# Batch norm with ReLU: the first half of x loaded and stored in pieces of 1, 1, 2, 4 and 8 rows per partition instead of 2, 2, 4 and 8

## The chip, the cores and the metric

One core of one Trainium2 chip; the sessions used different chips. The metric is the device time of one execution in microseconds. Timed runs of two kernels are taken in turns on the same chip. Executions of one kernel mostly lie within 0.3 us of each other.

## The reference

```python
batch, channels, h, w = 32, 128, 32, 32          # x: float32, 16.78 MB
normalized = (x - running_mean) / np.sqrt(running_var + eps)     # per channel
return np.maximum(normalized * gamma + beta, 0)
```

x is read once and the result written once, 33.56 MB in all. Per element there is one multiplication, one addition and a maximum.

## The kernel before

x is seen as 4096 rows of 1024 numbers, in two halves; each partition has 16 rows (J) of a half. A load brings some rows of every partition, 4 KB each and contiguous in memory; a store sends them back.

```python
J = 16
PIECES = (((0, 2), (2, 4), (4, 8), (8, 16)), ((0, 8), (8, 16)))
...
    for t in range(T):                              # T = 2 halves
        for a, b in PIECES[t]:
            xt = data.tile([P, b - a, HW], F32, name=f"x{t}_{a}")
            nc.sync.dma_start(out=xt, in_=xr[t, :, a:b, :])
            tiles.append((t, a, b, xt))
    raw = params.tile([Q, 4, J], F32, name="raw")
    for k, src in enumerate((running_var, gamma, running_mean, beta)):
        nc.scalar.dma_start(out=raw[:, k, :], in_=src.rearrange("(q j) -> q j", j=J))
    ...                                             # matmul, sqrt, reciprocal: scale_t, bias_t
    for t, a, b, xt in tiles:
        for j in range(a, b):
            nc.scalar.activation(out=xt[:, j - a, :], in_=xt[:, j - a, :], func=ACTF.Relu,
                                 bias=bias_t[:, j : j + 1], scale=scale_t[:, j : j + 1])
        nc.scalar.dma_start(out=outr[t, :, a:b, :], in_=xt)
```

All pieces have their own buffers, so no load waits for a buffer (before loads of x, the sync engine waited only for the landings of gamma, 3.1 us, and of beta, 0.9 us). Loads are issued from the sync engine (SP), parameter loads and stores from the scalar engine (ACT).

## Time and profile before

| | before |
|---|---|
| median time, 6 runs | 84.27 us |
| span in the profile | 82.3 us |
| scalar engine busy | 38.2 us |
| first activation, first store issued | 9.38, 11.78 us |
| last load landed, last store issued | 51.2, 60.39 us |
| first and last data packet of the DMA engines | 1.81, 81.10 us |

Times inside a profile count from the span's start. In the 40 slices, a digit is the busy share in tenths; in the stretches, the last two columns are the mean busy share of the 16 DMA engines and what they moved in GB/s. A packet is counted, in slices and stretches alike, with all its time in the one in which it begins, so a share can pass 1. A line of a timeline gives start, length, engine, line of the kernel, operation, what is written <- what is read, and the count; in brackets stands how long the engine had been idle and what ended that. SPq and ACTq are the DMA issues of these engines. A load is called landed when the activation that waits for it is released, about 1 us after its last packet (51.2 and 50.2 us here). "Packet records" below are the trace's single DMA packets, each with queue, start, duration and size. A "packet" there is one contiguous row of a piece, so its size is the piece's rows times 4 KB (before: 256 load packets of 8 KB, 128 of 16 KB and 384 of 32 KB, and as many store packets).

### The profile page before, as it was taken

How to read it: one execution, taken by the hardware profiler on the slowest of the kernel's cores; microseconds unless marked ns; L12 is line 12 of the kernel's file. 1: busy time of each engine (PE TensorE's matmuls, PEld its weight loads, DVE VectorE, ACT ScalarE, POOL GpSimd, SP SyncE). 2: the span in 40 equal slices, each digit the busy share in tenths (PEclk: the TensorE clock that was granted, in tenths of full speed). 3: DMA queues.
4: the chain of work that ended last, by engine and by line, in shares of the span. 5: the costliest groups of instructions: out<-in, count | busy, mean ns of one | idle time of the engine just before them, and what ended most of it. 6: DMA issues, size and time to landing. Idle time of an engine off the chain costs nothing.

```text
span 82.3 us, 117 instructions
## 1 busy us (share of the span) xinstructions
PE 0.7 (1%) x2; PEld 0.5 (1%) x2; DVE 0.8 (1%) x5; ACT 38.2 (46%) x34; POOL 0.8 (1%) x6
## 2 busy tenths in 40 slices
PE   0003000000000000000000000000000000000000
PEld 0002000000000000000000000000000000000000
DVE  0000300000000000000000000000000000000000
ACT  0600599990009999509999401999930000000000
POOL 3000000000000000000000000000000000000000
DMA  2899999997998997997999898997998999799790
GB/s 36 315 431 486 398 486 398 462 430 319 462 526 351 462 430 327 582 430 319 446 510 446 382 382 374 518 478 303 494 494 366 414 510 446 319 510 478 303 494 0
DMA packets 1792, 33.56 MB, mean 408 GB/s; under 512 B 256, under 2 KB 256, under 8 KB 256
## 3 DMA queue, kind: packets, MB, share of 16 engines
q1 hardware_dynamic: 864, 16.78, 48.6%
q10 hardware_dynamic: 928, 16.78, 47.5%
HBM read 16.78 MB, written 16.78 MB: 408 GB/s over the span
## 4 chain that ended last, share of the span: by engine, by line
DMA 60%; ACT 10%; ACTq 1%; issue 1%
DMA x<-in_x_dram 53%; ACT x L92 10%; DMA raw<-in_beta_dram 6%; ACTq L57 1%
## 5 line engine op out<-in xcount | busy, mean ns | idle before, releaser
L92 ACT ACTIVATE x<-x,bias_t,scale_t 128x1024 f32<-128x1024 f32 x32 | 36.6, 1227 | 15.4 <-DMA x<-in_x_dram 14.4
L80 ACT ACT_TABLE_LOAD x1 | 1.3, 1283 | 2.7 <-issue 2.7
L80 ACT ACTIVATE std_t<-cols,eps_t 128x16 f32<-128x16 f32 x1 | 0.3, 273 | 4.1 <-PE cols L72 4.1
L72 PE MATMUL cols<-raw,rep 8*128 8x64 f32 x2 | 0.7, 428 | 7.4 <-DMA raw<-in_beta_dram 7.4
L72 PEld LDWEIGHTS cols<-raw,rep 8*128 8x128 f32 x2 | 0.5, 306 | 7.4 <-issue 7.4
L62 POOL TENSOR_SCALAR_AFFINE_SELECT rep<-rep 8x128 f32<-8x128 f32 x1 | 0.4, 393 | 0.1
L82 DVE RECIPROCAL rstd_t<-std_t 128x16 f32<-128x16 f32 x1 | 0.3, 253 | 7.5 <-ACT std_t L80 7.5
L61 POOL MEMSET rep<- 8x128 f32 x1 | 0.2, 194 | 0.3 <-POOLq L116 0.3
L84 DVE TENSOR_TENSOR scale_t<-cols,rstd_t 128x16 f32<-128x16 f32 x1 | 0.2, 175 | 0.1
L86 DVE TENSOR_TENSOR ms_t<-cols,scale_t 128x16 f32<-128x16 f32 x1 | 0.2, 175 | 0.0
L88 DVE TENSOR_TENSOR bias_t<-cols,ms_t 128x16 f32<-128x16 f32 x1 | 0.2, 175 | 0.0
L116 POOL MEMSET const-bfloat16-1.0<- 128x1 bf16 x1 | 0.1, 106 | 0.0
L116 POOL MEMSET const-uint8-127<- 128x1 uint8 x1 | 0.1, 106 | 0.0
L116 POOL MEMSET const-float32-0.0<- 128x1 f32 x1 | 0.1, 103 | 0.3 <-issue 0.3
L116 POOL MEMSET const-float32-1.0<- 128x1 f32 x1 | 0.1, 103 | 0.0
L59 DVE MEMSET eps_t<- 128x1 f32 x1 | 0.1, 59 | 0.9 <-PEq L116 0.9
## 6 DMA issues: line engine op xcount, KB each, us to landing
x<-in_x_dram SPq DMA_DIRECT2D x3, 4096.0 KB, 22.7
out_dram<-x ACTq DMA_DIRECT2D x3, 4096.0 KB, 21.0
x<-in_x_dram SPq DMA_DIRECT2D x2, 1024.0 KB, 6.0
x<-in_x_dram SPq DMA_DIRECT2D x1, 2048.0 KB, 11.4
out_dram<-x ACTq DMA_DIRECT2D x2, 1024.0 KB, 25.9
out_dram<-x ACTq DMA_DIRECT2D x1, 2048.0 KB
raw<-in_running_var_dram ACTq DMA_DIRECT2D x1, 0.5 KB
raw<-in_gamma_dram ACTq DMA_DIRECT2D x1, 0.5 KB
```

The costliest lines, as they stand in the source:

```text
L57: nc.scalar.dma_start(out=raw[:, k, :], in_=src.rearrange("(q j) -> q j", j=J))
L59: nc.vector.memset(eps_t, float(eps))
L61: nc.gpsimd.memset(rep, 1.0)
L62: nc.gpsimd.affine_select(out=rep, in_=rep, compare_op=mybir.AluOpType.is_equal, fill=0.0, base=0, pattern=[[0, P // Q], [-1, Q]], channel ...
L72: nc.tensor.matmul(cols.rearrange("p k j -> p (k j)"), rep.rearrange("q r s -> q (r s)"), raw.rearrange("q k j -> q (k j)"), start=True, s ...
L80: nc.scalar.activation(out=std_t, in_=cols[:, 0, :], func=ACTF.Sqrt, bias=eps_t[:, 0:1], scale=1.0)
L82: nc.vector.reciprocal(out=rstd_t, in_=std_t)
L84: nc.vector.tensor_mul(out=scale_t, in0=cols[:, 1, :], in1=rstd_t)
L86: nc.vector.tensor_mul(out=ms_t, in0=cols[:, 2, :], in1=scale_t)
L88: nc.vector.tensor_sub(out=bias_t, in0=cols[:, 3, :], in1=ms_t)
L92: nc.scalar.activation(out=xt[:, j - a, :], in_=xt[:, j - a, :], func=ACTF.Relu, bias=bias_t[:, j : j + 1], scale=scale_t[:, j : j + 1],)
L116: nc = _bacc.Bacc("TRN2", target_bir_lowering=False, num_devices=1)
```

## The change

The intent: the first piece lands sooner, its activation and its store start sooner, and loads and stores run side by side for longer.

```diff
-PIECES = (((0, 2), (2, 4), (4, 8), (8, 16)), ((0, 8), (8, 16)))
+PIECES = (((0, 1), (1, 2), (2, 4), (4, 8), (8, 16)), ((0, 8), (8, 16)))
```

## The prediction

That the two queues take turns packet by packet is read from the trace of the kernel before: gamma, mean and beta landed at 5.98, 6.62 and 7.26 us, about two packets of 0.309 us apart, and beside 32 KB load packets the first store's 8 KB packets began in groups about 1.5 us apart (16.00, 17.53, 19.11, 20.63 us).

> **What bounds the kernel now.** I read the page first: the engine totals, the 40 slices, the chain; then the timeline of the scalar engine, the busy time by stretches, and last the records of single DMA packets, because the page pointed to the DMA. The page, and the chain that ended last:
>
> ```profile
> PE 0.7 (1%) x2; PEld 0.5 (1%) x2; DVE 0.8 (1%) x5; ACT 38.2 (46%) x34; POOL 0.8 (1%) x6
> ...
> ACT  0600599990009999509999401999930000000000
> POOL 3000000000000000000000000000000000000000
> DMA  2899999997998997997999898997998999799790
> ...
> HBM read 16.78 MB, written 16.78 MB: 408 GB/s over the span
> ...
> DMA 60%; ACT 10%; ACTq 1%; issue 1%
> ```
>
> The scalar engine, the only compute engine with work, is idle for more than half of the span; the DMA row shows no gap from the second slice (2 us) to the last but one (80 us). The chain runs through a DMA most of the time. The stretches say whether the DMA engines ever had nothing to do (columns: stretch, length, busy time of PE, PEld, DVE, ACT and POOL, clock, DMA share, GB/s; a packet is booked where it ends, so a share can pass 1):
>
> ```profile
> 2.00:10.00 8.00, 0.66 (x2) 0.49 (x2) 0.78 (x4) 2.17 (x3) 0.00 (x0) 1.00 1.00 413
> 10.00:16.00 6.00, 0.00 (x0) 0.00 (x0) 0.00 (x0) 6.00 (x6) 0.00 (x0) 1.00 0.96 400
> 16.00:37.00 21.00, 0.00 (x0) 0.00 (x0) 0.00 (x0) 11.70 (x12) 0.00 (x0) 1.00 1.04 443
> 37.00:51.20 14.20, 0.00 (x0) 0.00 (x0) 0.00 (x0) 9.16 (x8) 0.00 (x0) 1.00 0.97 412
> 51.20:60.40 9.20, 0.00 (x0) 0.00 (x0) 0.00 (x0) 9.16 (x8) 0.00 (x0) 1.00 1.05 454
> 60.40:80.00 19.60, 0.00 (x0) 0.00 (x0) 0.00 (x0) 0.00 (x0) 0.00 (x0) 1.00 1.00 431
> 80.00:82.30 2.30, 0.00 (x0) 0.00 (x0) 0.00 (x0) 0.00 (x0) 0.00 (x0) 1.00 0.00 0
> ```
>
> The share is 0.96 to 1.05 in every stretch from 2 to 80 us, whether only loads run (up to 16 us), both (to 51 us) or only stores (after), and the rate does not depend on which. So loads and stores share one budget, and **the kernel is bound by its DMA engines from the first packet to the last**. The packet records give the budget exactly. Each piece is 128 packets, 8 on each of 16 engines, one per partition. Loads and stores take the same time for the same size (median): 8 KB 0.309 us, 16 KB 0.611 us, 32 KB 1.213 us. One engine's loads are 8 x (2 x 0.309 + 0.611 + 3 x 1.213) = 38.9 us; with the stores 77.9 us. The first data packet starts at 1.8 us, the last ends at 81.1 us: 79.3 us, of which only 1.4 us is anything but packets at their usual pace (slow first packets, some slower 32 KB reads).
>
> The scalar engine's timeline shows when stores are issued:
>
> ```profile
> 9.38 3.50 ACT L92 ACTIVATE x<-x,bias_t,scale_t 128x1024 f32<-128x1024 f32 x3 [1.03 <-DVE bias_t L88]
> 11.78 0.38 ACTq L99 DMA_DIRECT2D out_dram<-x  x1
> ...
> 37.00 1.24 ACT L92 ACTIVATE x<-x,bias_t,scale_t 128x1024 f32<-128x1024 f32 x1 [2.97 <-DMA x<-in_x_dram]
> 37.00 0.34 ACTq L99 DMA_DIRECT2D out_dram<-x  x1
> ...
> 51.21 1.24 ACT L92 ACTIVATE x<-x,bias_t,scale_t 128x1024 f32<-128x1024 f32 x1 [5.05 <-DMA x<-in_x_dram]
> 51.21 0.34 ACTq L99 DMA_DIRECT2D out_dram<-x  x1
> ...
> 60.39 0.34 ACTq L99 DMA_DIRECT2D out_dram<-x  x1
> ```
>
> The first activation starts at 9.38 us, released by bias_t, the end of the parameter chain; the first piece of x had landed at 5.7 us. So the size of the first piece is not what holds the first activation. A store also comes just after the first activation of the next piece, so two stores (37.00, 51.21) wait 3 and 5 us for the next load; that costs nothing, as the DMA is busy with loads.
>
> [...] 33.56 MB in 79.3 us is 423 GB/s, a steady 32 KB packet gives 16 x 32768 B / 1.213 us = 432 GB/s, for loads and stores together. [...] beside 32 KB loads, an 8 KB store packet should get one turn in 0.309 + 1.213 = 1.52 us, so 8 turns take 12.2 us; the first store's packets run from 16.0 to 27.6 us (11.6 us). [...]
>
> **The change, part by part.** It replaces one 1 MB load by two of 512 KB, and one 1 MB store likewise. Every byte still moves once, the activations stay 32 of 1.225 us.
>
> Packets: 4 KB ones were never measured here. The three sizes lie on a line: 0.302 us for 8 KB more, 0.602 us for 16 KB more, which leaves 0.007 us per packet. So a 4 KB packet is estimated at 0.158 us. Per engine, 8 packets of 8 KB (2.47 us) become 16 of 4 KB (2.53 us): +0.06 us for the load, +0.06 us for the store, and 2 completion packets of 0.009 us: **+0.13 us on the path that sets the end.**
>
> Issues: one more on the sync queue (about 0.43 us) and one more on the scalar queue (0.34 us). The loads' issues (0.43 us apart) stay ahead of the 512 KB pieces' transfer (8 x 0.158 = 1.3 us each), so no engine runs dry. Hidden.
>
> Parameters: the four parameter loads take turns with packets of x. Gamma, mean and beta land 0.64 us apart, which is two turns behind 8 KB packets each. Behind 4 KB packets they come sooner; beta, now at 7.3 us, I expect at 5 to 6.8 us, the first activation at 7 to 9 us instead of 9.38, the first store, now one activation later instead of two, at 8.3 to 10.2 us instead of 11.78. That is the intended effect, about 2.5 us. It is not on the path: until the loads end, an earlier store packet only takes a turn from a load packet.
>
> Loads and stores between: small store packets get fewer bytes per turn. Before, some 16 packets of 8 KB and 5.4 of 16 KB (8.2 us per engine) went out before the last load packet ended at 50.2 us. Now each of about 22 remaining 32 KB load packets shares with a store packet: 16 of 0.158 and 6 of 0.309 us, 4.4 us. So the last load should land some 3.8 us sooner, at about 47.4 us instead of 51.2, and the last store be issued at about 56.6 instead of 60.39 us. **This gain is not kept**: the bytes that the stores did not move by then remain to be moved. After the loads (46.4 us), 38.97 + 0.06 - 4.4 = 34.6 us of store packets remain, which ends at 81.0 us plus small gaps, as now. And the store queue cannot run dry: when the loads end, about 15 us of earlier stores are queued (a few of the 2-row piece, the 4-row piece 4.9 us, the 8-row piece 9.7 us), the next store is issued within a microsecond, and the last one 10 us later.
>
> Sum: 84.28 + 0.13 = **84.4 us**.
>
> **The rivals.** (1) *The earlier start shortens the end.* If the store stream were a pipeline of its own, with its own bandwidth, a store 2.5 us earlier would give 81.8 us (3% faster). For it: the change was made for that. Against it: the DMA share of 0.96 to 1.05 in all stretches and the same 0.309 and 1.213 us in both directions; a third of the time in load-only and store-only phases would leave room if directions were separate, and the rate does not rise when both run. (2) *Small packets are slow.* If a 4 KB packet took as long as an 8 KB one, the 32 added packets' worth would cost 2 x 8 x 0.15 = 2.4 us: 86.8 us, 3% slower. For it: never measured here[...]. Against it: the 0.007 us intercept. (3) *A new wait on a reused semaphore.* The fifth and sixth loads wait for the landing of parameter loads (issued at 6.00 and 7.27 us), since the kernel seems to have eight DMA semaphores. One more load and one more store shift these pairs; a store that waits for a late load would hold the scalar queue. With 10 us or more of queued packets behind every issue after 7 us this would have to be a very long wait: perhaps 0 to 1 us. (4) *The first microseconds.* The first packet of x took up to 1.17 us instead of 0.31 us; with half-size packets such a start-up could be a few tenths better or worse.
>
> **Range and chances.** Rivals 1 and 2 each need a linear or a saturated row of this trace to break: 1.5% each. Rivals 3 and 4 move the time by tenths; the three runs before spread over 0.3 us. So 84.0 to 84.9 us eight times in ten; faster by over 2% 0.015, within 2% 0.97, slower by over 2% 0.015.
>
> **What would show it.** Right: DMA share near 1 in all stretches from 2 to 80 us; 4 KB packets near 0.16 us; first store before 10.5 us; last load landing near 47.4 and last store issue near 56.6 us, and yet the last packet at 81 us. Wrong: a hole in the DMA row (rival 3), 4 KB packets well above 0.16 us (rival 2)[...].

## The result

The changed kernel's median is 84.41 us (84.15 to 84.48, 6 runs) against 84.27 us (84.13 to 84.46, 6 runs): ratio 1.001, 95% interval 0.999 to 1.003. In a second comparison in a later session (below) it was 1.0028 (1.0012 to 1.0044). So the change gains nothing; by the medians it costs 0.14 and 0.20 us, and only the second is clear of noise.

From the page of the changed kernel: the activity of ACT and DMA in 40 slices, and the chain that ended last.

```profile
ACT  0600489993019999289995099993000000000000
...
DMA  1999999897979697969889799998999899799980
...
DMA 55%; ACT 10%; issue 1%; SPq 1%; ACTq 0%
```

The last busy slice of ACT moved from the 30th to the 28th (two slices are 4 us): the scalar engine is done sooner. The DMA row still ends in the 39th. The changed kernel's stretches, with the same columns and bounds as those of before:

```profile
2.00:10.00 8.00, 0.66 (x2) 0.50 (x2) 0.78 (x4) 1.95 (x3) 0.00 (x0) 1.00 1.00 385
10.00:16.00 6.00, 0.00 (x0) 0.00 (x0) 0.00 (x0) 5.55 (x6) 0.00 (x0) 1.00 1.05 453
16.00:37.00 21.00, 0.00 (x0) 0.00 (x0) 0.00 (x0) 14.17 (x13) 0.00 (x0) 1.00 0.99 422
37.00:51.20 14.20, 0.00 (x0) 0.00 (x0) 0.00 (x0) 11.38 (x11) 0.00 (x0) 1.00 1.01 436
...
60.40:80.00 19.60, 0.00 (x0) 0.00 (x0) 0.00 (x0) 0.00 (x0) 0.00 (x0) 1.00 1.00 431
```

No stretch has a hole. In the first the share is 1.00, as before, but only 385 GB/s moved instead of 413: the packets take longer there (0.83 us of excess per engine against 0.44 us, in the budget below). The scalar engine's timeline:

```profile
9.61 2.37 ACT L92 ACTIVATE x<-x,bias_t,scale_t 128x1024 f32<-128x1024 f32 x2 [1.02 <-DVE bias_t L88]
10.88 1.50 ACTq L99 DMA_DIRECT2D out_dram<-x  x2
...
47.30 1.24 ACT L92 ACTIVATE x<-x,bias_t,scale_t 128x1024 f32<-128x1024 f32 x1 [2.82 <-DMA x<-in_x_dram]
...
56.48 0.34 ACTq L99 DMA_DIRECT2D out_dram<-x  x1
```

The first store is issued 0.9 us sooner, the last load lands 3.9 us sooner, the last store is issued 3.9 us sooner, and the last data packet ends at 81.11 us instead of 81.10. What the middle gained is given back at the end, where the stores that did not go out earlier still have to go out. The profiled run was the fastest of the six (84.15 us); in the second profile (84.63 us) the last load landed at 48.04 us, the last store was issued at 57.23 us and the last packet ended at 81.59 us.

An early issue is also not an early store: the first store's first packet began at 14.85 us, 4.0 us after the issue (before: 16.00 us, 4.2 us after). In e6 below, where the loads had just ended, it was 0.9 us (41.19 to 42.07 us).

### The profile page after: what moved, and what is told of

It reads as the page before. It is cut to its first block, busy times and chain, and to the rows that moved or that the text cites. A ratio compares the mean times of both kernels' runs of the same rounds, so it can differ in the third digit from the quotient of the medians.

```text
span 82.4 us, 121 instructions
## 1 busy us (share of the span) xinstructions
PE 0.7 (1%) x2; PEld 0.5 (1%) x2; DVE 0.8 (1%) x5; ACT 38.3 (46%) x34; POOL 0.8 (1%) x6
## 3 DMA queue, kind: packets, MB, share of 16 engines
q10 hardware_dynamic: 1072, 16.78, 47.4%
## 4 chain that ended last, share of the span: by engine, by line
DMA 55%; ACT 10%; issue 1%; SPq 1%; ACTq 0%
DMA x<-in_x_dram 55%; ACT x L92 10%; SPq L50 1%; ACTq L99 0%
```

## The experiments

**Theory:** the end is the start of the first packet, plus the time of all packets of one DMA engine, plus the stalls of packets, plus the holes in which the engines have nothing. When a store or an activation starts matters only if it opens a hole. **Rivals:** (R1) stores run as a stream of their own, so their start matters; (R2) what happens beside the loads is hidden, only the part after the last load counts; (R3) the number of transfers or the activations set the end.

### e1: the first half's stores held back by 22 us (from the changed kernel)

```diff
+    held = []
     for t, a, b, xt in tiles:
         for j in range(a, b):
-            nc.scalar.activation(...)
-        nc.scalar.dma_start(out=outr[t, :, a:b, :], in_=xt)
+            act = nc.scalar.activation(...)
+            if held and t == 1:
+                with tc.issue_after(act.ins):
+                    for o, i in held:
+                        nc.scalar.dma_start(out=o, in_=i)
+                held = []
+        if t == 0:
+            held.append((outr[t, :, a:b, :], xt))
+        else:
+            nc.scalar.dma_start(out=outr[t, :, a:b, :], in_=xt)
```

> The changed kernel with the same pieces, but all stores of the first half of x held back until after the first activation of the second half, so that the first store is issued at about 33 us instead of 10.9 us. Theory (the DMA engines' packet time alone sets the end): no hole arises, because the last load still runs; the loads end sooner (last landing near 43 us), the stores follow back to back, time 84.3 to 84.6 us, within 0.3% of the kernel before. Rival (the moment of the first store matters, stores form a stream of their own): the stores start 22 us later, so the end comes well later, above 90 us.

Measured: 85.03 us (84.94 to 85.09, 4 runs), before 84.20; ratio 1.0092 (1.0077 to 1.0107). The first store was issued at 33.07 us:

```profile
33.01 1.24 ACT L93 ACTIVATE x<-x,bias_t,scale_t 128x1024 f32<-128x1024 f32 x1 [0.55 <-DMA x<-in_x_dram]
33.07 2.35 ACTq L103 DMA_DIRECT2D out_dram<-x  x5
```

R1 falls: 22 us of delay cost 0.6 us against the changed kernel's 84.41 (another session). But 0.6 us is outside what the theory expected. The packet records show the 32 KB load packets 0.59 us per engine slower than their usual 1.213 us in total, all of it between 35 and 45 us, after these stores were issued; in the changed kernel it was 0.14 us. There is no hole.

### e2: the opposite of the change, the first half in two pieces of 8 rows (from the kernel before)

```diff
-PIECES = (((0, 2), (2, 4), (4, 8), (8, 16)), ((0, 8), (8, 16)))
+PIECES = (((0, 8), (8, 16)), ((0, 8), (8, 16)))
```

> The opposite of the change: the first half of x in two pieces of 8 rows, as the second half. First store near 23 us instead of 11.8. Theory: 24 packets fewer of 8 and 16 KB per engine and direction, replaced by 32 KB ones: 8 x (1.229 - 1.213) = 0.13 us less per direction, so 84.0 us (83.8 to 84.3), no hole. Rival (the first store's moment matters): 8 to 11 us slower.

Measured: 84.99 us (84.87 to 85.09, 4 runs), ratio 1.0087 (1.0071 to 1.0103). The first store came at 24.06 us, 12 us later than before, and cost 0.8 us, not 8 to 11. Again R1 falls, and again the theory's figure was too low by about 1 us. Its stretches around the first store:

```profile
24.00:26.00 2.00, 0.00 (x0) 0.00 (x0) 0.00 (x0) 1.54 (x3) 0.00 (x0) 1.00 1.40 524
26.00:28.00 2.00, 0.00 (x0) 0.00 (x0) 0.00 (x0) 2.00 (x3) 0.00 (x0) 1.00 0.95 246
28.00:30.00 2.00, 0.00 (x0) 0.00 (x0) 0.00 (x0) 2.00 (x2) 0.00 (x0) 1.00 0.69 295
```

Packets are booked where they begin, so take the three together: the share is (1.40 + 0.95 + 0.69) / 3 = 1.01, so the engines were busy, but they moved (524 + 246 + 295) / 3 = 355 GB/s. The records show why: load packets that began between 25.4 and 27.6 us took up to 1.8 us longer than 1.213 us, 1.17 us per engine in all. So in this kernel load packets stall after the first store's issue at 24.06 us and before its first packet at 28.79 us. The share of busy time hides it; the rate shows it.

### e3: 4 KB packets for every transfer (from the kernel before)

```diff
-            xt = data.tile([P, b - a, HW], F32, name=f"x{t}_{a}")
+            xt = data.tile([P, b - a, HW + 16], F32, name=f"x{t}_{a}")[:, :, :HW]
```

> The kernel before with its own pieces, but with 64 bytes of padding behind each row of x in the on-chip buffers, so that every transfer goes in 4 KB packets. Same transfers, same waits, same activations. Theory: 256 packets of 0.159 us per engine and direction are 40.7 us against 38.94, so 3.5 us more: 87.8 us (87.3 to 88.6), 4% slower. Rival (the end is set by the number of transfers, their issue or the activations): 84.3 us. Rival (small packets cost more in bulk than the first 16 per engine showed): above 89 us.

Measured: 86.43 us (86.35 to 86.49, 4 runs), ratio 1.0258 (1.0243 to 1.0273). Same transfers and activations, 2.2 us slower: the packets' time sets the end, and R3 falls. But the expected 3.5 us were too many. Its stretches, first with loads and stores, then with stores alone:

```profile
20.00:60.00 40.00, 0.00 (x0) 0.00 (x0) 0.00 (x0) 18.56 (x17) 0.00 (x0) 1.00 1.02 421
62.00:82.00 20.00, 0.00 (x0) 0.00 (x0) 0.00 (x0) 6.91 (x7) 0.00 (x0) 1.00 1.02 422
```

and the kernel before with stores of 32 KB packets alone:

```profile
62.00:79.00 17.00, 0.00 (x0) 0.00 (x0) 0.00 (x0) 0.00 (x0) 0.00 (x0) 1.00 1.00 432
```

A steady share of 1.02 says that recorded packets overlap by some 2%: a 4 KB packet is recorded with 0.159 us but one follows the other every 16 x 4096 B / 422 GB/s = 0.155 us. At 422 instead of 432 GB/s, 33.55 MB need 79.5 instead of 77.7 us, 1.8 us more; that is most of the 2.2 us. The step that failed was to multiply recorded durations by the count.

### e5: the first two stores left out (from the kernel before; wrong result)

```diff
-        nc.scalar.dma_start(out=outr[t, :, a:b, :], in_=xt)
+        if (t, a) not in ((0, 0), (0, 2)):
+            nc.scalar.dma_start(out=outr[t, :, a:b, :], in_=xt)
```

> Wrong result on purpose: the kernel before without its first two stores (rows 0 to 3 of the first half, 2 x 1 MB, never written). Theory: these stores' 16 packets of 0.309 us per engine are on the path that sets the end although they go out beside loads in the first half of the span: 4.94 us less, 79.3 us (79.0 to 79.6). Rival (stores beside loads are hidden, only what comes after the last load counts): 84.3 us.

Measured: 80.92 us (80.79 to 81.17, 4 runs), ratio 0.9611 (0.9587 to 0.9634), so 3.3 us less. R2 falls: these 2 MB go out beside loads, before 40 us, and taking them away shortens the end. The missing 1.6 us are a hole, in the stretches around 57 us:

```profile
50.00:56.00 6.00, 0.00 (x0) 0.00 (x0) 0.00 (x0) 0.00 (x0) 0.00 (x0) 1.00 1.01 437
56.00:57.00 1.00, 0.00 (x0) 0.00 (x0) 0.00 (x0) 0.00 (x0) 0.00 (x0) 1.00 0.02 0
57.00:58.00 1.00, 0.00 (x0) 0.00 (x0) 0.00 (x0) 0.67 (x1) 0.00 (x0) 1.00 0.00 0
58.00:59.00 1.00, 0.00 (x0) 0.00 (x0) 0.00 (x0) 1.00 (x2) 0.00 (x0) 1.00 1.22 524
```

```profile
57.33 1.24 ACT L92 ACTIVATE x<-x,bias_t,scale_t 128x1024 f32<-128x1024 f32 x1 [10.19 <-DMA x<-in_x_dram]
57.39 0.34 ACTq L100 DMA_DIRECT2D out_dram<-x  x1
```

The store of the second 4 MB piece stands in the scalar engine's queue behind the first activation of the last piece, which waits until 57.33 us for its load. All earlier stores were done by then, so the DMA engines idled (1.6 us of all engines, by the records). Expected gain 4.94 us less 1.6 us is 3.3 us, as measured. (Load packets also stalled 0.4 us more than before, 0.98 against 0.56 us; terms of 0.1 to 0.3 us at the start and the end offset most of that.) This is the same queue order that cost nothing in the kernel before, where stores stood behind waits of 2.97 and 5.05 us; here, where the store queue ran dry, it cost the 1.6 us.

### e4: the parameter loads ahead of x on the sync queue (from the kernel before)

```diff
+    raw = params.tile([Q, 4, J], F32, name="raw")
+    for k, src in enumerate((running_var, gamma, running_mean, beta)):
+        nc.sync.dma_start(out=raw[:, k, :], in_=src.rearrange("(q j) -> q j", j=J))
     tiles = []
...
-    raw = params.tile([Q, 4, J], F32, name="raw")
-    for k, src in enumerate((running_var, gamma, running_mean, beta)):
-        nc.scalar.dma_start(out=raw[:, k, :], in_=src.rearrange("(q j) -> q j", j=J))
```

> The kernel before with the four parameter loads moved from the scalar engine's queue to the sync engine's, ahead of the loads of x. The parameters land some microseconds sooner (by about 4 us instead of 7.3), so the first activation starts as soon as the first piece of x lands, near 7.5 us instead of 9.4; but the first load of x is issued about 1.5 us later. Theory (first x packet + packet time = end): 1.3 to 1.7 us slower, 85.8 us. Rival (the start of the activations and of the stores counts): up to 2 us faster, 82.5 us.

Measured: 85.61 us (85.40 to 85.77, 4 runs), before 84.21; ratio 1.0165 (1.0146 to 1.0185), so 1.4 us more. Its timeline:

```profile
2.24 5.17 SPq L53 DMA_DIRECT2D x<-in_x_dram  x6
...
7.15 3.63 ACT L92 ACTIVATE x<-x,bias_t,scale_t 128x1024 f32<-128x1024 f32 x3 [2.80 <-DMA x<-in_x_dram]
```

The activations start 2.2 us sooner than before (7.15 against 9.38 us), yet the kernel is slower by just what the first load is later: 2.24 - 0.81 = 1.43 us. The first data packet moved from 1.81 to 3.22 us, 1.41 us.

### e6: each half in one piece of 16 rows (from the kernel before)

```diff
-PIECES = (((0, 2), (2, 4), (4, 8), (8, 16)), ((0, 8), (8, 16)))
+PIECES = (((0, 16),), ((0, 16),))
```

> Each half of x in one piece of 16 rows: two loads and two stores of 8 MB. The first store can be issued only when 16 activations are done after the first landing near 22 us, that is near 41 us, just when the loads end (40.8 us), and the second near 61 us, just when the first store's packets end. Theory: packet time falls by 0.3 us or more, but two holes of 0 to 1.5 us each in the DMA row can open: 84 to 86.5 us, and the packet records account for the difference as holes. If larger pieces only ever gain: 83.8 us. Rival (the first store's moment matters as such): over 100 us.

Measured: 83.70 us (83.61 to 83.88, 6 runs), before 84.21; ratio 0.9938 (0.9924 to 0.9953). The first store was issued at 41.19 us, 29 us later than before, and the kernel is 0.5 us faster. That is below the expected 84 to 86.5 us. Where the loads end:

```profile
41.00:42.00 1.00, 0.00 (x0) 0.00 (x0) 0.00 (x0) 0.16 (x1) 0.00 (x0) 1.00 0.01 0
42.00:43.00 1.00, 0.00 (x0) 0.00 (x0) 0.00 (x0) 0.80 (x1) 0.00 (x0) 1.00 2.45 1049
```

The records show one hole, between 41 and 43 us, worth 0.8 us, and not the second that was allowed for. After the start the load packets lose only 0.01 us, and loads and stores never meet (the first store packet began at 42.07 us, after the loads); that gain was not expected. (The profiled run, 83.88 us, was the slowest of the six, so its last packet, at 80.99 us, shows only part of the 0.5 us.)

### h1: loads of before, stores of after

```diff
+STORES = (((0, 1), (1, 2), (2, 4), (4, 8), (8, 16)), ((0, 8), (8, 16)))
...
     for t, a, b, xt in tiles:
-        for j in range(a, b):
-            nc.scalar.activation(...)
-        nc.scalar.dma_start(out=outr[t, :, a:b, :], in_=xt)
+        for c, d in STORES[t]:
+            if c < a or d > b:
+                continue
+            for j in range(c, d):
+                nc.scalar.activation(...)
+            nc.scalar.dma_start(out=outr[t, :, c:d, :], in_=xt[:, c - a : d - a, :])
```

> One half of the change: loads as before (2, 2, 4, 8 rows), stores as after (1, 1, 2, 4, 8 rows). What the runs so far suggest: each engine's load packets stall just before the first store packets, the more the larger that first store is (summed over time, per engine: 0.14 us with 512 KB in the changed kernel, 0.38 us with 1 MB before, 0.95 us with 2 MB, 1.17 us with 4 MB), and the first microseconds of the loads cost 0.44 us with 8 KB packets but 0.84 us with 4 KB ones. If so, this half keeps the gain alone: 0.2 us less than before, 83.9 to 84.1 us, excess of the load packets near 0.6 us. Rival (both are chance differences of single profiles): 84.2 to 84.3 us, as before.

Measured: 83.74 us (83.71 to 83.91, 6 runs), before 84.17; ratio 0.9946 (0.9923 to 0.9969). That is below the expected 83.9 to 84.1 us; the excess of the load packets, 0.57 us, was near the expected 0.6. The gain over the kernel before is clear of noise.

### h2: loads of after, stores of before

```diff
+LOADS = (((0, 1), (1, 2), (2, 4), (4, 8), (8, 16)), ((0, 8), (8, 16)))
...
-            nc.sync.dma_start(out=xt, in_=xr[t, :, a:b, :])
+            for c, d in LOADS[t]:
+                if a <= c and d <= b:
+                    nc.sync.dma_start(out=xt[:, c - a : d - a, :], in_=xr[t, :, c:d, :])
```

> The other half: loads as after (1, 1, 2, 4, 8 rows), stores as before (2, 2, 4, 8 rows). By the same theory this half keeps the loss alone: 0.4 us more than before, 84.5 to 84.7 us, start-up excess of the 4 KB load packets near 0.8 us. Rival (chance): 84.2 to 84.4 us.

Measured: 84.33 us (84.25 to 84.45, 6 runs), ratio 1.0010 (0.9989 to 1.0030). A miss: the loss at the start was there (0.81 us of excess), but the later excess, expected as before, was only 0.12 us.

### h3: the loads of e2 with the stores of after

```diff
-PIECES = (((0, 2), (2, 4), (4, 8), (8, 16)), ((0, 8), (8, 16)))
+PIECES = (((0, 8), (8, 16)), ((0, 8), (8, 16)))
+STORES = ...                                       # and the loop of h1
```

> Loads of the first half in two pieces of 8 rows as in the second experiment (84.99 us), but stores in pieces of 1, 1, 2, 4 and 8 rows. Theory (the stall at the first store grows with its size): the stall falls from 1.17 us to 0.1 to 0.4 us and the time to 84.0 to 84.3 us. Rival (any first store beside a load stream of 32 KB packets costs that stall): 84.9 to 85.0 us.

Measured: 84.37 us (84.19 to 84.51, 6 runs), ratio 1.0011 (0.9988 to 1.0033); e2 was at 1.0087, on another chip. The time is just above the expected range. The gain over e2 is there, 0.6 us. At the first store (19 to 21 us) the stall fell from 1.17 to about 0.22 us; another 0.61 us came between 41 and 44 us, in the last load packets, which the theory of a stall at the first store doesn't explain.

### e9: loads and stores kept apart, made to be the fastest

```diff
-PIECES = (((0, 2), (2, 4), (4, 8), (8, 16)), ((0, 8), (8, 16)))
+PIECES = (((0, 2), (2, 16)), ((0, 16),))
+STORES = (((0, 2), (2, 16)), ((0, 8), (8, 16)))
...                                                  # the loop of h1; the store of rows 0 and 1
+            with tc.issue_after(act.ins):           # queued behind the activation of row 15
+                for o, i in held:
+                    nc.scalar.dma_start(out=o, in_=i)
```

> A version meant to be the fastest: 64 KB packets nearly throughout, first load small, no store before about 39 us, when the loads are about to end, so that loads and stores hardly meet; the last store split so that it is issued in time. Theory: first packet at 1.8 us, 77.4 us of packets, 0.45 us at the start, 0.2 to 0.5 us where stores begin, no hole: 82.8 to 83.4 us, 1.0 to 1.6% faster than before, although its first store comes 27 us later. If the stores were held too long a hole opens at 41 us as in the run with whole halves: 83.7 us. Rival (late stores cost): above 84.5 us.

Measured: 84.54 us (84.49 to 85.12, 6 runs), ratio 1.0045 (1.0018 to 1.0073). It failed, in two ways that its timeline shows:

```profile
20.21 5.88 ACT L98 ACTIVATE x<-x,bias_t,scale_t 128x1024 f32<-128x1024 f32 x5 [1.02 <-DVE bias_t L90]
24.98 0.38 ACTq L110 DMA_DIRECT2D out_dram<-x  x1
26.00 12.53 ACT L98 ACTIVATE x<-x,bias_t,scale_t 128x1024 f32<-128x1024 f32 x11
```

By the kernel's text the store of rows 0 and 1 stands behind 16 activations, but it was issued when the fifth began, with 11 of the 16 still to start. (The trace doesn't record the order of the built program. But the semaphore wait of the second store, whose rows need all 16, ran at 25.41 us, with the same 11 to start.) So its place in the text did not make the store wait for those 16 activations, and stores met the loads after all. Nor did it go as soon as its own rows were done, at about 22.6 us (an estimate: 20.21 us plus 2.37 us, which two activations take in the changed kernel); why it went at 24.98 us isn't shown. And the parameter loads, taking turns with 56 KB packets, landed so late that the matmul that waits for beta started at 18.23 us and the first activation at 20.21 us. (How long such turns are, the records show later in this run: 8 KB store packets followed each other every 2.72 us beside 64 KB load packets of 2.418 us; 2.418 + 0.309 = 2.73.) The last load packet of each engine, begun after 40 us, took about 1 us longer than usual; the second store had been issued at 38.56 us, its first packet followed at 44.54 us. Whether its issue caused that isn't shown. The time touches the rival's range (above 84.5 us), but the run doesn't test that rival: the first store was not late. There is no hole, and the later stalls are 1.12 us against 0.56 us before.

### r_after, r_before: both kernels once more, on one chip

The edit is one comment line in each.

> The changed kernel once more, for a second profile and more timed runs on one chip with the kernel before. If the two sizes seen in single profiles are properties of the kernels, its load packets show again 0.7 to 0.9 us of excess at the start (4 KB packets) and 0.1 to 0.2 us after; time 84.3 to 84.5 us. If they are chance, the second number can be anything from 0.1 to 0.6 us.

> The kernel before once more, for a second profile. If its excess of 0.56 us in the 32 KB load packets (most of it at 14 to 22 us, where its first stores go out) belongs to it, it comes again, beside 0.4 to 0.5 us at the start. If it is chance, as the run with small loads and the stores of before (0.12 us) makes likely, it is somewhere else between 0.1 and 0.6 us. Time 84.1 to 84.4 us, ratio 1.000.

Measured: 84.39 us (84.22 to 84.70, 6 runs), ratio 1.0028 (1.0012 to 1.0044), for the changed kernel; 84.21 us (84.12 to 84.30, 4 runs), ratio 1.0004 (0.9990 to 1.0019), for the kernel before. The excesses came again in each, by the table below; only that of the kernel before at the start (0.29 us) was smaller than expected.

### The budget of one DMA engine

From the packet records, in us, mean of the 16 engines. "Usual" is each packet at the median duration of its size; excess is what load packets took beyond that, in the first 5 us and later; "rest" is the last packet's end less all the others: holes, overlaps and uneven engines. (The 0.88 us of "after again" is mostly engines that ended unevenly after 80 us.)

| kernel | first packet | usual | excess, start | excess, later | rest | last end |
|---|---|---|---|---|---|---|
| before | 1.81 | 77.89 | 0.44 | 0.56 | 0.41 | 81.10 |
| before again | 1.80 | 77.89 | 0.29 | 0.74 | 0.28 | 81.00 |
| after | 1.82 | 78.03 | 0.83 | 0.15 | 0.28 | 81.11 |
| after again | 1.79 | 78.03 | 0.78 | 0.11 | 0.88 | 81.59 |
| h1 | 1.81 | 77.96 | 0.40 | 0.17 | 0.23 | 80.57 |
| h2 | 1.80 | 77.96 | 0.81 | 0.12 | 0.33 | 81.01 |
| e6 | 1.81 | 77.47 | 0.71 | 0.01 | 0.99 | 80.99 |

The change adds 0.14 us of usual packet time, and the two excesses trade places: about 0.4 to 0.5 us more at the start, about 0.4 to 0.6 us less later. A start with two loads of 512 KB is dearer in all four profiles that have it (0.71 to 0.83 us: after twice, e1, h2) than one with a load of 1 MB in 8 KB packets in all six (0.29 to 0.50 us: before twice, h1, e4, e5, e9). The packet size alone is not the reason: e3 starts with 1 MB in 4 KB packets and has 0.37 us. Nor is a larger first load always cheaper: 4 MB had 0.52 and 0.53 us (e2, h3), 8 MB 0.71 us (e6). On what the later excess hangs isn't settled: the kernel before has it (0.56, 0.74), h1 and h2, which change only the stores or only the loads, don't (0.17, 0.12). The theory that it grows with the first store's size fits e2 (4 MB, 1.17 us), e5 (2 MB, 0.98 us) and h3's first store, and fails in h2, whose first store is that of before, and in e9, where load packets lost only 0.1 us at a first store of 1 MB.

## Why the prediction was right

- **The bound** (one budget of packet time for loads and stores, busy from 2 to 80 us). Right: e1, e2 and e6 moved the first store by 12 to 29 us, for -0.5 to +0.8 us. e5 took away early store packets and the end moved; e4 moved the first packet by 1.41 us and the time by 1.4 us.
- **The 4 KB packet, estimated at 0.158 us.** Recorded with 0.159 us. The sum of +0.13 us holds in the records (0.14 us). e3 shows that recorded durations overlap a little, so in bulk such a sum is too high; for 32 packets it made no visible difference.
- **The gain that is not kept.** Last load predicted at 47.4, seen at 47.3 us; last store issue predicted at 56.6, seen at 56.48 us; last packet at 81 us. The second profile has 48.04, 57.23 and 81.59 us, so the agreement to 0.1 us is partly luck; that the gain in the middle is given back shows in both.
- **The parameters: wrong.** They were to land at 5 to 6.8 us and the first activation to start at 7 to 9 us; the matmul that waits for beta started at 7.62 us instead of 7.39 before, the activation at 9.61 instead of 9.38, so the first store was issued at 10.88 us, outside 8.3 to 10.2. Gamma's packets did go out about 1 us sooner (4.0 to 4.4 instead of 5.0 to 5.3 us, by the records), beta's did not (5.7 to 6.8 instead of 6.3 to 6.6 us). The step that failed is "behind 4 KB packets": when beta's first packet went, at 5.72 us, 255 of the 256 load packets of 4 KB had already begun, and it followed the packets of running_mean by 0.63 us, as before; so beta took its turns beside 8 KB packets. Why its slowest packet came later still isn't known; in h2, with the same loads, beta's packets went at 5.8 to 6.1 us and the first activation started at 8.88 us. It was off the path, as the prediction said.
- **Rival 4, the first microseconds.** It was given a few tenths either way; it cost about 0.4 us. The time stayed within 0.2 us only because the later load packets lost less. The prediction had not foreseen this second term, so part of its closeness is two errors of about 0.4 us with opposite signs.
- **Rival 3, the semaphores.** In the trace the issues share eight semaphores in both kernels (16 issues before, 18 after), and before loads the sync engine waited 3.1 us for gamma and 0.9 us for beta in the kernel before, 2.8 us in two waits for x and 2.6 us for beta in the changed one. The last load was issued at 8.70 us instead of 7.27; no hole followed.
- **Slips in the working that the sum doesn't rest on.** Rival 2 should have cost twice as much: there are 16 packets of 4 KB per engine and direction, so 2 x 16 x 0.15 = 4.8 us, 89.1 us. Load-only and store-only phases are not a third of the time but over half of it (about 2 to 16 and 50 to 81 us). And packets are booked where they begin, not where they end: the last stretch of before, from 80 us, shows a share of 0.00 although packets ran until 81.10 us. So the rate of a single stretch depends on where its bounds fall, and the 443 GB/s in a mixed stretch before the change says nothing against the bound, 432 GB/s by the 32 KB packets.

No version beats the kernel before by more than 0.6%: h1 (83.74 us) and e6 (83.70 us), each measured beside it and not beside each other, are the best found.

## What to carry to other kernels

In these kernels the DMA engines were busy nearly from the first packet to the last and loads and stores shared their time; an earlier or later store changed the order of the packets and little of the time (the first store moved by 12 to 29 us for -0.5 to +0.8 us in e1, e2 and e6). Where a profile looks like this, ask first whether there is a hole that an earlier store would fill. Here the time was moved by the first packet's start (1.41 us in e4), by the usual packet time (most of 2.2 us in e3), by stalls of load packets (0.29 to 0.83 us at the start and, in most of these kernels, more before a store's first packet, 1.17 us in e2; what sets their size isn't settled), and by holes (1.6 us in e5), and each could be read off the packet records. A share of 1.0 does not rule out a stall: in e2 it was 1.01 at 355 GB/s. Look at the GB/s beside it.
